# Last f split inside the fifth group's projection, low weight passes last in each first tile, the residual in the output tensor with adding transfers, and a last token tile in three banks

## Chip, cores, metric

One of the eight cores of a Trainium2 chip runs the whole kernel. Its engines are TensorE (PE, matrix products into the accumulation banks of PSUM), VectorE (DVE), ScalarE (ACT) and GpSimd (POOL); SyncE (SP) issues most transfers, GpSimd a few. Every engine works its own list of instructions in order and waits on semaphores for the others. The metric is the time on the device in microseconds for one execution; less is better. The kernel before takes 1384.19 us, the median of three runs (1382.83 to 1386.5).

## The reference

One decoder layer on 1024 tokens of width 1024, float32. What bears on the change is the end: the residual x after the mixer, the convolutional feed-forward block with 2816 channels, and the last norm.

```python
x = x + rms_norm(merged @ w_out[l], norm_mix_post[l])

h = rms_norm(x, norm_ffn_pre[l])
u = causal_dwconv(h @ w_up[l], conv_ffn_w[l])
a, g = jnp.split(u, 2, axis=-1)
f = (jax.nn.gelu(g, approximate=True) * a) @ w_down[l]
x = x + rms_norm(f, norm_ffn_post[l])
```

`rms_norm(x, g)` is `x * rsqrt(mean(x*x) + 1e-6) * g` over the 1024 columns of a token.

## The kernel before

Products are made to nearly float32 accuracy from 16-bit pieces. A float32 tile t, scaled by a power of two s, is split into a high half (float16 of s t, an ACT copy at L86) and a low half (s t less the high half, a DVE operation at L87). A product of two split operands is three matmuls, high x high, high x low and low x high, in the order of `PASSES` = ((0,0), (0,1), (1,0)), the first index for f (or the moving side) and the second for w. The scale comes from a sum of squares over the operand: `scale_of` reduces it on DVE, casts it to bfloat16 (L69), sums it over the partitions by a matmul with one column (`pr`, L74) and shapes the power of two in three small DVE operations (L76 to L79).

The mixer writes the new residual x2 tile by tile, in eight token tiles of 128 x 1024, to a buffer in device memory (`x2d`, L861), about 600 us before the end. The feed-forward block goes through 22 pairs of channel blocks of 128 (an a and a g block each; their matmuls are L1137). What comes out of a pair is a tile `ua` of 128 channels x 1024 tokens. The pairs are gathered in six groups (`GROUPS` = 2, 4, 4, 4, 4, 4), and for each group g there are three steps:

- `f_split(g)` finds the scale over the group's tiles and splits each into `f16` halves (four ACT passes, four DVE passes).
- `dn_split(g)` loads the group's rows of `w_down` (`wd`, L1005) and splits them into `wdh`. Its loads go through four buffers that other weight loads share, so that a load waits until an earlier tile has been split.
- `down(g)` multiplies: for each of eight token tiles and each of two halves of 512 columns, it takes an accumulation bank and runs 3 x GROUPS[g] matmuls (L1036) into it; then the bank is added on DVE to `yacc` (L1042; for the first group ACT copies it, L1040). There are eight banks, shared with the pairs' products and the scales.

`down(g-1)` is called while the pairs of group g are made. At the end come `down(4)`, then `f_split(5)`, then `down(5)`. In the last group each token tile is also finished: ACT squares and sums each half of `yacc` (L1044), DVE multiplies it by the gain (L1046), the two sums are added (L1048), `rstd` makes mean + eps on DVE (L170) and the power of -1/2 on POOL (L171), DVE forms o * r + x2 in two halves (L1052), with x2 loaded back by SP (`x2r`, L1029), and SP stores each half (L1053).

The order of the instructions on each engine is not quite that of the program. A scheduler arranges them when the kernel is built: it takes the program's order as the priority (with some sections raised), and a model of the durations tells it which instruction is ready. In the trace the matmuls of the first tiles of a group are therefore spread over several banks. The order is fixed once the kernel is built; on the chip each engine keeps to it and waits. Large working tiles of the end (`f16`, `wdh`, `ua`, `o`, `x2r`, the gain) share sixteen buffers of 4 KB per partition.

Of the kernel before, what the change touches and what calls it, by code (L numbers as in the profile page):

```python
# [18 lines left out]
F32 = mybir.dt.float32  # L19
I32 = mybir.dt.int32  # L20
AF = mybir.ActivationFunctionType
ALU = mybir.AluOpType
AX = mybir.AxisListType

P = 128
T = 1024
D = 1024
KD = D // P
NH = 512
# [3 lines left out]
GROUPS = (2, 4, 4, 4, 4, 4)  # L33
KH = KD // 2
PASSES = ((0, 0), (0, 1), (1, 0))


class Layer:
# [225 lines left out]
    def mixer(self, mid):  # L264
        tc, nc, a = self.tc, self.nc, self.a
# [446 lines left out]
        with ExitStack() as ph2:  # L712
# [81 lines left out]
            for d in range(1, 8):  # L794
                p = gp[d]
# [37 lines left out]
        self.hA = hA = self.hp.tile([P, 2, KD, T], F16, tag="hT", name="hA")  # L833
        self.hB = hB = self.h7p.tile([P, 2, 3, KH, NH], F16, tag="hB", name="hB2")
        dram = self.top.enter_context(tc.tile_pool(name="dram", bufs=1, space=bass.MemoryType.DRAM))
        self.x2 = [dram.tile([P, D], F32, tag=f"x2_{tt}", name=f"x2d_{tt}") for tt in range(8)]
        gp = self.xp.tile([P, D], F32, tag="x", name="g_post")
        nc.gpsimd.dma_start(gp, a["g_mix_post"].broadcast_to([P, D]))
        gf = self.xp.tile([P, D], F32, tag="x", name="g_ffn")
# [144 lines left out]
    def ffn(self):  # L984
        tc, nc, a = self.tc, self.nc, self.a
        ff0 = self.ff0
        f16, invd, yacc, draw = {}, {}, [None] * 8, self.dsums
        ng = len(GROUPS)

        def f_split(g):  # L990
            smf, ft = smfs[g], fts[g]
            s, inv = self.scale_of(smf, GROUPS[g], keep=True)
            f16[g] = []
            for n, fo in enumerate(ft):
                t = self.slot([P, 2, T], F16, f"f16_{g}_{n}")
                self.split(t, fo, s, f"f{g}_{n}")
                f16[g].append(t)
            invd[g] = inv

        def dn_split(g, wh=False):  # L1000
            s, inv = self.scale_of(draw[g], GROUPS[g], keep=True)
            out = []
            for i in range(GROUPS[g]):
                t = self.ws.tile([P, D], F32, tag="ws", name=f"wd2_{g}_{i}")
                nc.sync.dma_start(t, a["w_down"][ff0[g] + i])  # L1005
                w = self.wh.tile([P, 2, D], F16, tag="wh", name=f"wdh_{g}_{i}") if wh else \
                    self.slot([P, 2, D], F16, f"wdh_{g}_{i}")
                self.split(w, t, s, f"dn{g}_{i}")
                out.append(w)
            draw[g] = out, inv  # L1010

        def down(g):
            w, inv = draw.pop(g)
            sm = self.small(f"sd{g}", keep=True)
            self.mul(sm[:, 0:1], invd[g], inv)
            last = g == ng - 1
            if last:
                gq = self.slot([P, D], F32, "g_ffn_post")
                nc.gpsimd.dma_start(gq, a["g_ffn_post"].broadcast_to([P, D]))
            for tt in range(8):  # L1020
                if g == 0:
                    yacc[tt] = (self.o16p.tile([P, D], F32, tag="o16", name=f"yacc{tt}") if tt < 4 else
                                self.xp.tile([P, D], F32, tag="x", name=f"yacc{tt}"))
                y = yacc[tt]
                if last:
                    o = self.slot([P, D], F32, f"o{tt}")
                    sm_ = self.small(f"fin{tt}")
                    x2 = self.slot([P, D], F32, f"x2r{tt}")
                    nc.sync.dma_start(x2, self.x2[tt])  # L1029
                for nh in range(2):  # L1030
                    ps = self.bank(f"pd{g}_{tt}_{nh}")
                    sl = ds(nh * NH, NH)
                    n = 0
                    for k in range(GROUPS[g]):
                        for hi, wi in PASSES:
                            nc.tensor.matmul(ps, f16[g][k][:, hi, ds(tt * P, P)], w[k][:, wi, sl],  # L1036
                                             start=n == 0, stop=n == 3 * GROUPS[g] - 1)
                            n += 1
                    if g == 0:
                        nc.scalar.activation(y[:, sl], ps, AF.Copy, scale=sm[:, 0:1])  # L1040
                    else:
                        nc.vector.scalar_tensor_tensor(y[:, sl], ps, sm[:, 0:1], y[:, sl], ALU.mult, ALU.add)  # L1042
                    if last:
                        nc.scalar.activation(self.junk(f"jf{tt}_{nh}")[:, sl], y[:, sl], AF.Square,  # L1044
                                             accum_out=sm_[:, 3 + nh:4 + nh])
                        nc.vector.tensor_tensor(o[:, sl], y[:, sl], gq[:, sl], ALU.mult)  # L1046
                if last:
                    nc.vector.tensor_tensor(sm_[:, 0:1], sm_[:, 3:4], sm_[:, 4:5], ALU.add)  # L1048
                    r = self.rstd(sm_)
                    for e in range(2):  # L1050
                        sl = ds(e * NH, NH)
                        nc.vector.scalar_tensor_tensor(o[:, sl], o[:, sl], r, x2[:, sl], ALU.mult, ALU.add)  # L1052
                        nc.sync.dma_start(a["out"][ds(tt * P, P), sl], o[:, sl])  # L1053

        smfs = [self.small(f"sm_f{g}", keep=True) for g in range(ng)]
        fts = [[] for _ in range(ng)]
        prs = self.pairs

        def finish(f):
            g = max(g for g in range(ng) if ff0[g] <= f)  # L1060
            fts[g].append(prs[f].finish(smfs[g][:, f - ff0[g]:f - ff0[g] + 1]))

        for g in range(ng):
            for n in range(GROUPS[g]):
                f = ff0[g] + n
                p = prs[f]
                begun = n == 2 and 1 <= g < ng - 1
                if f >= 1 and not begun:
                    if f >= 2:
                        p.prod(1)  # L1070
                    prs[f - 1].prod(4)
                if f >= 1 and f + 1 < NFF:
                    self.pair_split(f"u{f + 1}")
                if 1 <= f and f + 2 < NFF:
                    self.pair_fetch(f"u{f + 2}")
                if f >= 1 and not begun:
                    finish(f - 1)
                p.prod(6)
                if f >= 2:
                    p.prod(5)  # L1080
                if f >= 2:
                    p.prod(2)
                p.prod(7)
                if n == 1 and g >= 1:
                    f_split(g - 1)
                    if g < ng - 1:
                        dn_split(g - 1)
                p.prod(3)
                if f == 0:
                    self.pair_sums("u2")  # L1090
                if n == 1 and 1 <= g < ng - 1:
                    prs[f + 1].prod(1)
                    p.prod(4)
                    finish(f)
                    down(g - 1)
                if f >= 1 and f + 2 < NFF:
                    self.pair_sums(f"u{f + 2}")
                if n == 2:
                    self.dn_sums(GROUPS[g])
        dn_split(ng - 2)  # L1100
        prs[NFF - 1].prod(4)
        finish(NFF - 1)
        dn_split(ng - 1, True)
        down(ng - 2)
        f_split(ng - 1)
        down(ng - 1)


# [158 lines left out]
```

## Time and profile before

| what | value |
|---|---|
| median of three runs | 1384.19 us (1382.83 to 1386.5) |
| the profiled execution | 1386.05 us |
| span of its instructions | 1384.3 us |
| TensorE occupied | 1340.9 us (97%) |
| VectorE, ScalarE, GpSimd | 1052.5, 836.7, 28.6 us |
| matmuls of the down projection (L1036) | 1056, 232.5 us |
| mean granted TensorE clock | 0.996 |

Times in the profile are microseconds from the start of the span. Occupied time of TensorE counts overlapping matmuls once; a matmul of 512 columns is listed with 379 ns, though another can start about 216 ns after it. A figure in square brackets at the end of a row of the timeline is the time for which the engine sat idle before that row, and what released it. The granted clock is the share of full speed that the power control gave TensorE.

### The profile page before, as it was taken

To read this page: it belongs to the slowest core of one execution; us is meant where nothing else is said; L and a number is where in the kernel's file an instruction comes from. 1 tells how busy PE (TensorE), PEld (TensorE's weight loads), DVE (VectorE), ACT (ScalarE), POOL (GpSimd) and SP (SyncE) were. 2 spreads that over 40 slices of the span, in tenths; PEclk is the share of its full clock that TensorE was granted. 3 is DMA by queue.
4 is the path that set the end of the run, shared out by engine and by line. 5 is a ranking of instruction groups with operands and counts; after the bars stand their busy time and mean duration, and the time that the engine had idled before them with its cause. 6 is when DMAs were issued, how large, how long until landed. Compare 5 with 4: busy or idle time off the path is not lost. (4 is left out here: it accounts for less than half of the span.)

```text
span 1384.3 us, 17016 instructions
## 1 busy us (share of the span) xinstructions
PE 1340.9 (97%) x6639; PEld 607.1 (44%) x6639; DVE 1052.5 (76%) x1646; ACT 836.7 (60%) x1169; POOL 28.6 (2%) x45
## 2 busy tenths in 40 slices
PE   6999999999989999999999999999999999999997
PEld 3444444444434444444454444444444444444443
DVE  5667777776684797878788886985995796699757
ACT  6668777786864465666466576652762662567422
POOL 2000000000000000000010000000000000000001
PEclk9999999999999999999999999999999999999999
DMA  7102111111111112351341223122120322312125
GB/s 260 62 1 61 31 34 39 35 31 31 31 31 46 31 31 61 91 183 39 114 135 49 61 61 122 47 76 91 62 91 3 119 61 62 122 46 107 61 71 188
DMA packets 28593, 99.74 MB, mean 72 GB/s; under 512 B 3296, under 2 KB 3424, under 8 KB 28512
## 3 DMA queue, kind: packets, MB, share of 16 engines
q1 hardware_dynamic: 28080, 97.08, 21.4%
q0 software_dynamic: 432, 1.57, 0.3%
q8 instruction: 52, 0.85, 0.2%
q14 instruction: 29, 0.24, 0.1%
HBM read 90.25 MB, written 8.39 MB: 71 GB/s over the span
## 5 line engine op out<-in xcount | busy, mean ns | idle before, releaser
L1137 PEld LDWEIGHTS <-wh_u 128*128 128x128 f16 x1848 | 178.7, 98 | 217.7 <-issue 4.0
L1036 PE MATMUL pd<-wdh,f 128*128 128x512 f16 x1056 | 232.5, 381 | 9.3 <-DVE wdh L87 5.1
L1036 PEld LDWEIGHTS <-f 128*128 128x128 f16 x1056 | 103.6, 98 | 136.4 <-issue 11.3
L86 ACT ACTIVATE wh_u<-ws_u,sc 128x1024 f16<-128x1024 f32 (+1 forms) x66 | 64.2, 998 | 101.6 <-DVE sc L78 82.0
L1042 DVE SCALAR_TENSOR_TENSOR yacc<-pd,sd,yacc 128x512 f32<-128x512 f32 x80 | 58.7, 748 | 68.1 <-PE pd L1036 60.7
L1137 PEld LDWEIGHTS <-wh_g 128*128 128x128 f16 x588 | 56.8, 98 | 71.5 <-ACT wh_g L86 2.3
L853 PE MATMUL py<-wh_wo,m 128*128 128x512 f16 x384 | 83.9, 379 | 0.0
L87 DVE SCALAR_TENSOR_TENSOR wh_u<-ws_u,sc,wh_u 128x1024 f16<-128x1024 f32 (+1 forms) x66 | 72.0, 1103 | 7.1 <-ACT wh_u L86 7.1
L625 DVE SCALAR_TENSOR_TENSOR w<-zc,w 128x1024 f16<-128x1024 f32 (+3 forms) x48 | 45.7, 955 | 32.0 <-ACT w L624 32.0
L582 PE MATMUL A<-sh,tri 128*128 128x512 f16 (+3 forms) x352 | 67.9, 322 | 0.7 <-DVE zc L620 0.7
L604 ACT ACTIVATE sp<-zc 128x1024 f32<-128x1024 f32 (+3 forms) x48 | 40.2, 838 | 46.4 <-DVE zc L597 29.1
L1214 DVE SCALAR_TENSOR_TENSOR ugu<-cgu,cw_g,ugu 128x1023 f32<-128x1023 f32 (+1 forms) x44 | 56.4, 1282 | 10.9 <-ACT ugu L1212 10.5
L1214 DVE SCALAR_TENSOR_TENSOR ua<-cau,cw_a,ua 128x1023 f32<-128x1023 f32 (+1 forms) x44 | 56.3, 1278 | 1.1 <-ACT ua L1212 1.0
L853 PEld LDWEIGHTS <-m 128*128 128x128 f16 x384 | 37.5, 98 | 44.1
L608 DVE TENSOR_TENSOR sh<-sp,sh 128x1024 f16<-128x1024 f32 (+3 forms) x48 | 45.8, 953 | 12.5 <-ACT sh L607 12.3
L622 ACT ACTIVATE zc<-zc 128x1024 f32<-128x1024 f32 (+3 forms) x48 | 40.1, 834 | 15.2 <-DVE zc L620 14.7
L620 DVE SCALAR_TENSOR_TENSOR zc<-A,zc 128x1024 f32<-128x1024 f32 (+3 forms) x48 | 45.6, 950 | 2.6 <-PE A L582 2.5
L1212 ACT ACTIVATE ua<-cau,cw_a 128x1024 f32<-128x1024 f32 x22 | 25.1, 1139 | 37.1 <-DVE cau L1164 33.9
L56 ACT ACTIVATE jk_u<-ws_u 128x1024 bf16<-128x1024 f32 x44 | 46.3, 1053 | 1.0 <-DMA ws_u<-w_up_nt 0.2
L200 PE MATMUL pk<-hT,wh_k 128*128 128x512 f16 x192 | 46.8, 380 | 0.0
L200 PE MATMUL pq<-hT,wh_q 128*128 128x512 f16 x192 | 44.3, 379 | 1.3 <-DVE sc L79 1.3
L565 PE MATMUL pywc<-p,wh_wc 128*128 128x512 f16 x192 | 43.4, 387 | 2.2 <-ACT p L86 1.6
(613 smaller groups left out, 2626.0 us busy)
## 6 DMA issues: line engine op xcount, KB each, us to landing
ws_u<-w_up_nt SPq DMA_DIRECT2D x44, 512.0 KB, 3.6
ds<-w_down SPq DMA_DIRECT2D x22, 512.0 KB, 6.1
wd<-w_down SPq DMA_DIRECT2D x22, 512.0 KB, 3.7
ws_g<-w_in_nt SPq DMA_DIRECT2D x14, 512.0 KB, 3.6
x<-x SPq DMA_DIRECT2D x8, 512.0 KB, 8.0
ws_wo<-w_out SPq DMA_DIRECT2D x8, 512.0 KB, 7.5
xr<-x SPq DMA_DIRECT2D x8, 512.0 KB, 4.1
x2d<-x SPq DMA_DIRECT2D x8, 512.0 KB, 2.9
```

The costliest lines, as they stand in the source:

```text
L56: self.nc.scalar.activation(self.junk(f"jk_{name}"), src, AF.Square, accum_out=acc)
L86: self.nc.scalar.activation(dst[:, 0, :], src, AF.Copy, scale=s)
L87: self.nc.vector.scalar_tensor_tensor(dst[:, 1, :], src, s, dst[:, 0, :], ALU.mult, ALU.subtract)
L200: nc.tensor.matmul(ps, w[:, wi, ds(k * P, P)], hT[:, hi, k, ds(c * NH, NH)], start=n == 0, stop=n == last)
L582: nc.tensor.matmul(out, w, mv, skip_group_check=True, **kw)
L608: nc.vector.tensor_tensor(sh[:, 1, :, off:], sp[:, :, off:], sh[:, 0, :, off:], ALU.subtract)
L625: nc.vector.scalar_tensor_tensor(w[:, 1, :, off:], zc[:, :, off:], 2.0 ** 14, w[:, 0, :, off:], ALU.mult, ALU.subtract)
L853: nc.tensor.matmul(ps, m16[k][:, hi, ds(tt * P, P)], wo[k][:, wi, sl], start=k == 0 and p == 0, stop=k == 7 and p == 2)
L1036: nc.tensor.matmul(ps, f16[g][k][:, hi, ds(tt * P, P)], w[k][:, wi, sl], start=n == 0, stop=n == 3 * GROUPS[g] - 1)
L1042: nc.vector.scalar_tensor_tensor(y[:, sl], ps, sm[:, 0:1], y[:, sl], ALU.mult, ALU.add)
L1137: nc.tensor.matmul(ps, w[wt][:, wi, ds(wc * NH + k * P, P)], self.block(i, hi, k), start=first and n == 0, stop=n == 3 * KH - 1, skip_grou ...
L1214: nc.vector.scalar_tensor_tensor(u[:, lag:], c[:, :T - lag], sm[:, 2 - lag:3 - lag], u[:, lag:], ALU.mult, ALU.add)
```

## The change

Four things are edited.

1. `f_split(5)` is no longer called between `down(4)` and `down(5)`, but inside `down(4)`, ahead of token tile 5.
2. In token tile 0 of every group, both halves' banks first take the passes with the high half of w for all weight tiles of the group (high f and low f), and then, in a second round, the passes with its low half. The other tiles keep the order of `PASSES`. Both banks of a tile are now taken before its matmuls.
3. The mixer writes x2 of token tiles 0 to 6 into the output tensor itself; tile 7 keeps a buffer of its own. At the end, tiles 0 to 6 are not loaded back: ACT multiplies o by r in one pass of 128 x 1024, and a transfer issued by GpSimd adds o to what stands in the output.
4. In the last group, token tile 7 uses three banks, of 512, 256 and 256 columns, and its three sums of squares are added by one reduction.

```diff
-        self.x2 = [dram.tile([P, D], F32, tag=f"x2_{tt}", name=f"x2d_{tt}") for tt in range(8)]
+        self.x2 = [a["out"][ds(tt * P, P), :] for tt in range(7)] + \
+            [dram.tile([P, D], F32, tag="x2_7", name="x2d_7")]
...
-        def down(g):
+        def down(g, between=None):
...
             for tt in range(8):
+                if between:
+                    between(tt)
...
-                    x2 = self.slot([P, D], F32, f"x2r{tt}")
-                    nc.sync.dma_start(x2, self.x2[tt])
-                for nh in range(2):
-                    ps = self.bank(f"pd{g}_{tt}_{nh}")
-                    sl = ds(nh * NH, NH)
-                    n = 0
-                    for k in range(GROUPS[g]):
-                        for hi, wi in PASSES:
-                            nc.tensor.matmul(ps, f16[g][k][:, hi, ds(tt * P, P)], w[k][:, wi, sl],
-                                             start=n == 0, stop=n == 3 * GROUPS[g] - 1)
-                            n += 1
+                    if tt == 7:
+                        x2 = self.slot([P, D], F32, f"x2r{tt}")
+                        nc.sync.dma_start(x2, self.x2[tt])
+                parts = [(0, NH), (NH, NH // 2), (NH + NH // 2, NH // 2)] if last and tt == 7 else [(0, NH), (NH, NH)]
+                pd = [self.bank(f"pd{g}_{tt}_{nh}")[:, :parts[nh][1]] for nh in range(len(parts))]
+                ks = range(GROUPS[g])
+
+                runs = [[(k, p) for k in ks for p in ((0, 0), (1, 0))], [(k, (0, 1)) for k in ks]] if tt == 0 else \
+                    [[(k, p) for k in ks for p in PASSES]]
+                for run in runs:
+                    for nh, part in enumerate(parts):
+                        for n, (k, (hi, wi)) in enumerate(run):
+                            nc.tensor.matmul(pd[nh], f16[g][k][:, hi, ds(tt * P, P)], w[k][:, wi, ds(*part)],
+                                             start=run is runs[0] and n == 0, stop=run is runs[-1] and n == len(run) - 1)
+                for nh, part in enumerate(parts):
+                    ps, sl = pd[nh], ds(*part)
...
-                    nc.vector.tensor_tensor(sm_[:, 0:1], sm_[:, 3:4], sm_[:, 4:5], ALU.add)
+                    if len(parts) == 2:
+                        nc.vector.tensor_tensor(sm_[:, 0:1], sm_[:, 3:4], sm_[:, 4:5], ALU.add)
+                    else:
+                        nc.vector.tensor_reduce(sm_[:, 0:1], sm_[:, 3:6], AX.X, ALU.add)
                     r = self.rstd(sm_)
+                    if tt < 7:
+                        nc.scalar.activation(o, o, AF.Copy, scale=r)
+                        nc.gpsimd.dma_start(a["out"][ds(tt * P, P), :], o, accum_op=ALU.add)
+                        continue
...
-        down(ng - 2)
-        f_split(ng - 1)
+        down(ng - 2, lambda tt: tt == 5 and f_split(ng - 1))
         down(ng - 1)
```

## The prediction

> **What bounds the kernel now.** I read the page's engine totals first, then who TensorE waits for, then its timeline around those waits, and last the tail behind the final matmul.
>
> ```profile
> PE 1340.9 (97%) x6639; PEld 607.1 (44%) x6639; DVE 1052.5 (76%) x1646; ACT 836.7 (60%) x1169; POOL 28.6 (2%) x45
> ```
>
> TensorE is occupied 1340.9 of 1384.3 us, so time comes only from its 43 us of idle, from its clock, or from the ends of the span. The waits of TensorE (engine line waited for: total us, times, longest) at the down projection's matmul, L1036, are:
>
> ```profile
> PE pd L1036 <- DVE wdh L87: 5.1, 5, 1.6
> PE pd L1036 <- ACT f L86: 2.3, 1, 2.3
> PE pd L1036 <- DVE cau L1164: 1.5, 1, 1.5
> PE pd L1036 <- ACT wdh L86: 0.4, 1, 0.4
> ```
>
> All four belong to starts of a group: the first projects no further until weights or f are split. The 2.3 us is the last group's. The timeline (start, duration, engine, line, operation, tiles, count, idle before and releaser) shows it:
>
> ```profile
> 1290.45 39.87 PE L1036 MATMUL pd<-wdh,f 128*128 128x512 f16 x184 [0.19 <-DVE wdh L87]
> ...
> 1301.36 1.28 DVE L87 SCALAR_TENSOR_TENSOR wdh<-wd,sc,wdh 128x1024 f16<-128x1024 f32 x1 [0.20 <-ACT wdh L86]
> ...
> 1307.70 0.15 DVE L69 CAST rb<-sc 128x1 bf16<-128x1 f32 x1
> ...
> 1328.69 0.58 POOL L1019 DMA_DIRECT2D g_ffn_post<-g_ffn_post  x1 [589.11 <-DVE yacc L1042]
> ...
> 1330.16 0.17 PE L74 MATMUL pr<-rb,ones 128*128 128x1 bf16 x1
> 1331.40 4.27 ACT L86 ACTIVATE f<-ua,sc 128x1024 f16<-128x1024 f32 x4 [25.13 <-DVE sc L78]
> 1332.58 4.87 DVE L87 SCALAR_TENSOR_TENSOR f<-ua,sc,f 128x1024 f16<-128x1024 f32 x4 [0.96 <-ACT f L86]
> 1332.61 43.30 PE L1036 MATMUL pd<-wdh,f 128*128 128x512 f16 x192 [2.27 <-ACT f L86]
> ```
>
> The input of the last f split is complete at 1307.85 (1307.70 + 0.15), yet its one-column matmul stands behind the whole of the fifth group in TensorE's order, so the splits begin at 1331.40 and TensorE idles 2.27 us. The stretches around that gap (us, busy time of each engine, granted clock, share of the DMA engines, GB/s) show a second price:
>
> ```profile
> 1330.33:1332.61 2.28, 0.01 (x2) 0.01 (x1) 1.22 (x6) 1.21 (x2) 0.00 (x0) 1.00 1.02 296
> 1332.61:1336.46 3.85, 3.85 (x10) 1.41 (x11) 3.85 (x4) 3.06 (x3) 0.00 (x0) 0.56 0.77 301
> 1336.46:1375.91 39.45, 39.45 (x183) 17.70 (x181) 31.45 (x58) 10.12 (x28) 4.61 (x7) 1.00 0.45 150
> ```
>
> After 2.28 us of idle the clock is granted at 0.56 for 3.85 us; then it is full again. At 1.00, 183 matmuls in 39.45 us are 0.2156 us each, and the fifth group's 184 in 39.87 agree (0.2167).
>
> **The change, part by part.**
>
> *The last f split moves into the fifth group.* Its instructions stay the same: one reduce, one cast, one one-column matmul, four small DVE operations, four ACT passes (4.27 us) and four DVE passes (4.87 us). They now start ahead of token tile 5, at about 1290.45 + 5 x 24 x 0.216 = 1316.4, after the cast of 1307.85, so the one-column matmul waits for nothing. ACT is empty there (the 25.13 us of idle in its row), and DVE evicts 0.75 us in every 2.59 us. The split is done near 1323, seven us ahead of the last group; cover for it is tiles 5 to 7 (15.5 us of matmuls). Without that cover it would cost again what it costs now. What is removed: the 2.27 us gap, and the slow clock behind it: 43.30 us less 192 x 0.2156 + 0.16 for the pipeline's fill (41.56) = 1.74. Together **4.0 us**. What is late next is nothing: the last group's weights were split by 1302.6 (1301.36 + 1.28), and its buffers come from those free before.
>
> The page TensorE: Matmul & The Clock Gate of the Trainium skill (Part 1, "What's actually happening") puts the fall to half rate after an idle window of about 3.4 us. By that figure a gap of 2.28 us would not slow the clock and only 2.3 us would be won; the trace's 0.56 behind a 2.28 us gap decides against it here.
>
> *Low w passes last, in the first token tile of each group.* The start of the fourth group:
>
> ```profile
> 1136.21 2.17 ACT L86 ACTIVATE wdh<-wd,sc 128x1024 f16<-128x1024 f32 x2
> 1138.14 1.46 PE L1036 MATMUL pd<-wdh,f 128*128 128x512 f16 x6
> 1139.90 1.28 DVE L87 SCALAR_TENSOR_TENSOR wdh<-wd,sc,wdh 128x1024 f16<-128x1024 f32 x1
> 1141.24 5.99 PE L1036 MATMUL pd<-wdh,f 128*128 128x512 f16 x27 [1.64 <-DVE wdh L87]
> ...
> 1144.95 1.15 ACT L86 ACTIVATE wdh<-wd,sc 128x1024 f16<-128x1024 f32 x1 [1.92 <-DMA wd<-w_down]
> 1146.13 1.28 DVE L87 SCALAR_TENSOR_TENSOR wdh<-wd,sc,wdh 128x1024 f16<-128x1024 f32 x1 [0.47 <-ACT wdh L86]
> ```
>
> Six matmuls, I read one in each of six banks, and then 1.64 us until the low half of the first weight tile is there. After the change the first tile's two banks take both passes of the first two weight tiles: 8, plus 4 in other banks, 12 x 0.216 = 2.59 us, to 1140.73; 0.5 us of wait is left to 1141.2. But the low passes of that tile now queue behind high passes of weight tiles three and four, whose load lands only at 1144.95 and whose high half is there at 1146.10. Of the 36 matmuls on two weight tiles in six banks, 32 remain in front: 1138.14 + 0.5 + 6.91 = 1145.55, a new wait of 0.5. Won: 1.64 - 1.0 = 0.6. The other groups start so:
>
> ```profile
> 813.87 0.38 PE L1036 MATMUL pd<-wdh,f 128*128 128x512 f16 x1 [1.47 <-DVE cau L1164]
> 815.06 4.04 PE L1036 MATMUL pd<-wdh,f 128*128 128x512 f16 x18 [0.82 <-DVE wdh L87]
> ...
> 909.41 17.00 PE L1036 MATMUL pd<-wdh,f 128*128 128x512 f16 x78 [0.80 <-DVE wdh L87]
> ...
> 1025.33 17.00 PE L1036 MATMUL pd<-wdh,f 128*128 128x512 f16 x78 [1.65 <-DVE wdh L87]
> ```
>
> The 0.80 can go whole (six extra matmuls are 1.3 us); the 1.65 is the twin of the 1.64 and gives 0.7; the first group gives two matmuls, 0.4, since a bank is what it waits for first; the fifth's 0.19 goes. Sum 0.8 + 0.7 + 0.6 + 0.4 + 0.2 = **2.7 us**. Bounds: 0 (an order of issue that does not use the freedom) to 5.1 (all waits for a low half); a loss is the second rival.
>
> *The tail.* The chain behind the last matmul, which ends at 1375.91:
>
> ```profile
> 1374.04 1.42 DVE L1052 SCALAR_TENSOR_TENSOR o<-o,fin,x2r 128x512 f32<-128x512 f32 x2 [0.73 <-POOL fin L171]
> 1374.82 6.38 SPq L1053 DMA_DIRECT2D out<-o  x4
> 1375.37 0.75 DVE L1042 SCALAR_TENSOR_TENSOR yacc<-pd,sd,yacc 128x512 f32<-128x512 f32 x1
> ...
> 1376.76 0.75 DVE L1042 SCALAR_TENSOR_TENSOR yacc<-pd,sd,yacc 128x512 f32<-128x512 f32 x1
> ...
> 1377.60 0.63 ACT L1044 ACTIVATE jf<-yacc 128x512 bf16<-128x512 f32 x1 [0.67 <-DVE yacc L1042]
> ...
> 1379.43 1.42 DVE L1052 SCALAR_TENSOR_TENSOR o<-o,fin,x2r 128x512 f32<-128x512 f32 x2 [0.73 <-POOL fin L171]
> ```
>
> Tile 7's first half is evicted only at 1375.37, because DVE holds tile 6's final pass, which waited for POOL; its bank was full at 1375.91 - 2.59 = 1373.32. So the second half goes out 0.85 us late. For tiles 0 to 6 that pass moves to ACT as one 128x1024 multiplication, and the x2r loads leave SP. The last bank has 256 columns. Rows for the smaller forms (busy, mean ns):
>
> ```profile
> L335 DVE SCALAR_TENSOR_TENSOR v<-pv,v 128x256 f16<-128x256 f32 x16 | 6.0, 418 | 5.8 <-ACT v L333 5.8
> L1212 ACT ACTIVATE ua<-cau,cw_a 128x1024 f32<-128x1024 f32 x22 | 25.1, 1139 | 37.1 <-DVE cau L1164 33.9
> L56 ACT ACTIVATE jk_u<-ws_u 128x1024 bf16<-128x1024 f32 x44 | 46.3, 1053 | 1.0 <-DMA ws_u<-w_up_nt 0.2
> 250.19 1.26 PE L582 MATMUL A<-sh,tri 128*128 128x256 f16 x8
> ```
>
> The eviction takes 0.42 to 0.75; I take 0.45, near the first. The square then starts 0.55 after the last matmul instead of 1.69 (1377.60 - 1375.91): 1.14 won. The square falls from 0.63 to 0.42 by the slope between 512 and 1024 columns (0.63, 1.05): 0.21. The three-column sum replaces a two-operand one of 0.16; equal. Against that, 24 matmuls of 256 columns: the row's eight give (1.26 - 0.27)/7 = 0.141 us a step where half of 0.216 would be 0.108, so 0 to 0.8, and I take 0.4. Net **0.95 us**.
>
> *Adding transfers.* None is in this trace. Near it stand:
>
> ```profile
> x2d<-x SPq DMA_DIRECT2D x8, 512.0 KB, 2.9
> x2r<-x2d SPq DMA_DIRECT2D x8, 512.0 KB, 3.8
> out<-o SPq DMA_DIRECT2D x16, 256.0 KB, 2.1
> g_ffn_post<-g_ffn_post POOLq DMA_DIRECT2D x1, 512.0 KB, 6.3
> ```
>
> An add moves 512 KB in and out: from 2.9 (a plain write) to 9.2 (POOL queue's 6.3 plus a write). Tile 6 ends on TensorE at 1375.91 - 5.18 = 1370.73; with tile 7's steps it is normed at 1370.73 + 0.85 + 1.83 = 1373.41, scaled by 1374.55. Tile 7's output, issued at 1374.82 + 6.38 - 0.33 = 1380.87, lands at 1383.0 now and 1382.05 then, so the add has 7.5 us. Between 2.9 and 9.2 I take 7.8, nearest to 3.8 + 2.9 on the POOL queue: **0.3 us lost**. On POOL the next tile's power operation stands behind the add's issue (an issue there took 0.58 us) and is ready only some 2 us later, so it is not held. The writing of x to the output instead of another buffer costs nothing: the same 2.9 us transfer, waited for by nobody for 600 us.
>
> **Sum:** 4.0 + 2.7 + 0.95 - 0.3 = 7.35 us. The profiled execution took 1386.05 us (span 1384.3 and 1.7 around it), 1.9 over the median 1384.19 and inside the runs' spread of 1382.83 to 1386.5. On it the sum gives 1378.7; on the mean of these four times, 1384.9, it gives **1377.6**, which I forecast.
>
> **Rivals.** (1) *The split order wins nothing at the group starts*, since the order of issue had already spread over six banks; speaks for it: only six matmuls were in hand in spite of the many that the program offers. Then 4.65 remain: 1380.3. (2) *The run of high passes becomes the wait*: issued as written, TensorE does 8 matmuls (to 1139.87) and waits for weight tile three until 1146.1, 6.2 us in place of 1.64, and a gap of that length brings the slow clock, 1.7 more. Three groups lose 3 x (4.6 + 1.7) = 19 less the 4.65: 1399. It is slower than before from a gap of some 3.2 us per start, or 2.3 with the slow clock. Against it: 78 matmuls in 17.00 us without a gap, although the third weight tile came late, so the order follows arrivals now. (3) *The adds run behind*: they pass one queue, 5.18 us apart. Over 5.2 us of the queue each, they pile up; the first is issued near 1339 (1330.3 + 5.2 for tile 0 + 3.8 for its norm and scaling, as in tile 6), so seven end at 1339 + 7x + 1.3, and from x = 6.3 the kernel is slower; at 9.2, 1405. Against it: 16 engines moved 301 GB/s above, so 1 MB takes 3.5 us. (4) *One add lags*: at 9.2 it ends 1.7 us after tile 7's output; 1379.3 with the other terms, 1380.7 with half of the group starts.
>
> **Chances.** Forecast 0.53 (its own range 1375 to 1379.5), rival 1 0.20, rival 4 0.14, rival 2 0.08, rival 3 0.05. A measurement of this kernel tells about 0.3% from no change, that is 1380.0 to 1388.3. Faster: 0.53 + half of rival 1 + 0.6 of rival 4 = 0.71; slower: most of rivals 2 and 3, 0.11; the same 0.18. Low end 1373.5: all of the 5.1 us won, no loss at 256 columns or adds, on the runs' lower half; high end 1382.5: rival 1 with the lagging add and the runs' upper half.
>
> **What would show it.** The profile after should have no wait of TensorE for ACT's f, clock 1.00 through the last group, a tail of 7 to 7.5 us where it is 8.4 now, group starts whose waits for the low halves shrink from 5.1 us, and adds that land in under 7.5 us. A wait of more than 3 us at a start, for weight tile three, or adds over 9 us would prove me wrong.

## The result and the profile after

The changed kernel takes 1375.89 us, the median of five runs (1373.96 to 1376.65), where the kernel before takes 1384.19 (1382.83 to 1386.5, by now also of five). The ratio is 0.9933, with a 95% interval of 0.992 to 0.9947: 9.3 us less, 7.3 to 11.1. The forecast was 1377.6, with 7.35 us won, in a range of 1373.5 to 1382.5, and 0.71 for faster. In a later comparison on one chip the same kernel gave 0.9934 (0.9922 to 0.9946).

TensorE's waits of the changed kernel (engine, line waited for, total us, times, longest) at the down projection, which is L1043 now:

```profile
PE pd L1043 <- ACT wdh L86: 1.2, 2, 0.7
PE pd L1043 <- DVE cau L1178: 1.0, 1, 1.0
PE pd L1043 <- DVE wdh L87: 0.6, 1, 0.6
```

The wait for ACT's f is gone, and the waits for low halves of w fell from 5.1 us to 0.6. Those for high halves rose from 0.4 to 1.2, since the first group now waits 0.69 us for a high half where it waited 0.82 for a low one. In all 9.3 us of waits at this line became 2.8. The timeline of the changed kernel around the split and the end (start, duration, engine, line, operation, tiles, count, idle before):

```profile
1283.99 26.06 PE L1043 MATMUL pd<-wdh,f 128*128 128x512 f16 x120 [0.47 <-ACT wdh L86]
...
1309.89 0.17 PE L74 MATMUL pr<-rb,ones 128*128 128x1 bf16 x1
1309.92 20.45 PE L1043 MATMUL pd<-wdh,f 128*128 128x512 f16 x94
...
1311.13 4.26 ACT L86 ACTIVATE f<-ua,sc 128x1024 f16<-128x1024 f32 x4 [8.87 <-DVE sc L78]
...
1317.22 1.27 DVE L87 SCALAR_TENSOR_TENSOR f<-ua,sc,f 128x1024 f16<-128x1024 f32 x1
...
1329.77 37.32 PE L1043 MATMUL pd<-wdh,f 128*128 128x512 f16 x184
```

The one-column matmul now runs after 120 matmuls of the fifth group, and the last low half of f is done at 1318.49 (1317.22 + 1.27), some 7 us ahead of the last group. TensorE has no gap from 1283.99 to 1367.09. The stretches of the changed kernel (us, busy time of each engine, granted clock, DMA share, GB/s) say the same of the clock, and give the tail:

```profile
1309.90:1367.09 57.19, 57.19 (x278) 26.93 (x276) 34.86 (x61) 22.89 (x43) 10.71 (x15) 1.00 0.41 74
1367.09:1374.20 7.11, 0.00 (x0) 0.00 (x0) 2.64 (x6) 0.51 (x2) 0.56 (x1) 0.66 0.69 148
```

The clock is 1.00 through the last group, and 7.11 us lie behind the last matmul where there were 8.39. The distances between the first matmuls of the groups, in the timelines of both kernels, show where the rest came from. The third column is the second experiment below.

| stretch, us | before | changed | low passes alone |
|---|---|---|---|
| first to second group's start | 96.00 | 95.43 | 95.46 |
| second to third | 115.07 | 114.11 | 114.11 |
| third to fourth | 115.92 | 114.18 | 114.18 |
| fourth to fifth | 150.24 | 149.17 | 149.19 |
| fifth group's start to the last matmul | 87.53 | 83.10 | 87.17 |
| tail | 8.39 | 7.11 | 8.48 |

The first four rows fell by 4.34 us, the fifth by 4.43, the tail by 1.28. At the first group's start the two executions stand level (811.15 and 811.10), though by different ways: the changed one had a stretch at half clock near 744 us (below), and the one before had come there 1.7 us later. That is 10.05 us on the profiled executions; the medians differ by 8.3.

### The profile page after: what moved, and what is told of

It reads as the page before. It is cut to its first block, busy times and chain, and to the rows that moved or that the text cites. A ratio compares the mean times of both kernels' runs of the same rounds, so it can differ in the third digit from the quotient of the medians.

```text
span 1374.2 us, 17008 instructions
## 1 busy us (share of the span) xinstructions
PE 1339.9 (98%) x6651; PEld 608.3 (44%) x6651; DVE 1044.3 (76%) x1634; ACT 844.3 (61%) x1178; POOL 34.2 (2%) x52
## 3 DMA queue, kind: packets, MB, share of 16 engines
HBM read 86.58 MB, written 8.39 MB: 69 GB/s over the span
## 5 line engine op out<-in xcount | busy, mean ns | idle before, releaser
L1043 PE MATMUL pd<-wdh,f 128*128 128x512 f16 (+1 forms) x1068 | 230.3, 377 | 2.8 <-ACT wdh L86 1.2
L1043 PEld LDWEIGHTS <-f 128*128 128x128 f16 x1068 | 104.4, 98 | 127.1 <-issue 4.1
L1050 DVE SCALAR_TENSOR_TENSOR yacc<-pd,sd,yacc 128x512 f32<-128x512 f32 (+1 forms) x81 | 58.5, 741 | 72.5 <-PE pd L1043 65.0
L605 ACT ACTIVATE sp<-sp,one 128x1024 f32<-128x1024 f32 (+3 forms) x48 | 44.5, 928 | 0.8
```

What stands on the lines that cost most here:

```text
L1043: nc.tensor.matmul(pd[nh], f16[g][k][:, hi, ds(tt * P, P)], w[k][:, wi, ds(*part)], start=run is runs[0] and n == 0, stop=run is runs[-1] ...
```

## The experiments

**The f split alone.** On the kernel before:

```diff
-        down(ng - 2)
-        f_split(ng - 1)
+        down(ng - 2, lambda tt: tt == 5 and f_split(ng - 1))
```

> The kernel before with the last f split alone moved into the fifth group ahead of token tile 5. Theory (gap and clock): the 2.27 us wait before the last group goes, and with it the half clock behind it, so TensorE ends 4.0 us earlier and the time is about 1380.9 where before is 1384.9 (ratio 0.9971); the group starts and the tail stay (7.0 us of waits at L1036 for weights, tail 8.4 us). Rival (the gap alone): the slow matmuls behind the gap have another cause and stay, 2.3 us won (0.9983). Rival (a new wait): the split in the middle delays evictions, TensorE waits for a bank, nothing is won.

Measured: ratio 0.9977 (0.9967 to 0.9987), 3.2 us less (1.8 to 4.6). From the fifth group's start to the last matmul it takes 83.41 us instead of 87.53, 4.1 less; the group starts keep their distances. Its timeline (columns as above) has the last three tiles of the fifth group and the whole last group in one piece:

```profile
1314.84 0.17 PE L74 MATMUL pr<-rb,ones 128*128 128x1 bf16 x1
1314.86 57.14 PE L1038 MATMUL pd<-wdh,f 128*128 128x512 f16 x264
```

264 matmuls of 0.2156 us are 56.9. So nothing new is waited for. The tail fell too, from 8.39 to 7.80 us, which was not expected. Its rows show why: DVE starts tile 6's final pass 2.53 us ahead of the last matmul's end (1372.00), where it was 1.87 before, and evicts the second half of tile 7 only 0.19 us late and not 0.85.

```profile
1369.47 1.41 DVE L1054 SCALAR_TENSOR_TENSOR o<-o,fin,x2r 128x512 f32<-128x512 f32 x2 [0.66 <-POOL fin L171]
...
1372.19 0.74 DVE L1044 SCALAR_TENSOR_TENSOR yacc<-pd,sd,yacc 128x512 f32<-128x512 f32 x1
```

The interval of the times takes in both 4.0 and 2.3, so this run alone doesn't say whether the half clock counts.

**The low passes alone**, the new `runs` for token tile 0 with two banks for each tile:

```diff
+                runs = [[(k, p) for k in ks for p in ((0, 0), (1, 0))], [(k, (0, 1)) for k in ks]] if tt == 0 else \
+                    [[(k, p) for k in ks for p in PASSES]]
```

> The kernel before with the order of passes alone changed (low w passes last in token tile 0 of each group). Theory (12 matmuls in hand instead of 6 at each start): the waits for low halves shrink from 5.1 us to about 0.6 and the time falls by 4.4 to 4.6 us (ratio about 0.9968), as the distances between the group starts of the changed kernel show; the 2.3 us gap before the last group stays. What was predicted was 2.7. Rival (a new wait for weight tile three takes it back): 2.7 or less, with waits of TensorE for ACT wdh of about 0.5 us at three groups.

Measured: 0.9979 (0.997 to 0.9987), 2.9 us less (1.8 to 4.2). The profiled execution won 4.3 us at the starts, just as the changed kernel, and 0.36 us more in the fifth group: 4.65. TensorE's waits at the line are these (releaser: total us, times):

```profile
  ACT f L86: 2.3, 1
  ACT wdh L86: 1.2, 2
  DVE cau L1168: 1.0, 1
  DVE wdh L87: 0.6, 1
```

The gap of 2.3 us stays, the 5.1 us for low halves became 0.6. The start of the fourth group, in the changed kernel's timelines of TensorE and of ACT, shows the mechanism:

```profile
1134.82 2.75 PE L1043 MATMUL pd<-wdh,f 128*128 128x512 f16 x12
1138.12 15.70 PE L1043 MATMUL pd<-wdh,f 128*128 128x512 f16 x72 [0.55 <-DVE wdh L87]
...
1141.64 1.15 ACT L86 ACTIVATE wdh<-wd,sc 128x1024 f16<-128x1024 f32 x1 [1.73 <-DMA wd<-w_down]
```

Twelve matmuls instead of six run ahead of the wait, and 0.55 us of it are left. Both were predicted (12 and 0.5). What was predicted besides, a new wait of 0.5 us for weight tile three, is not there: 72 matmuls go on without a gap, though the tile's high half is there only at 1142.79. Seven banks are open and not six: 12 + 72 matmuls are seven times twelve, and so are the 6 + 78 of the kernel before (the prediction shows the 78 at the second and third group). The seventh takes six more matmuls on the first two weight tiles, so 38 were in hand and not 32; 38 x 0.216 + 0.55 is 8.8 us, and the tile came 8.0 us after the start. At the third group the wait is gone whole, though the prediction took it for the fourth's twin: the first low half is there 2.6 us after the group's start (3.1 in the kernel before), which is just what twelve matmuls last.

That the runs show 2.9 us and the profile 4.65 stays open. The interval, 1.8 to 4.2, holds the 2.7 that was predicted, but neither the 4.4 to 4.6 expected of this run nor what the profile shows. The mean granted clock over the eleven runs is 0.9949 where the kernel before has 0.9955, some 0.8 us by estimate; but the adding transfers alone (below), which take no work from TensorE, have 0.9966, so such means differ by as much for reasons that no run here shows.

**More high passes first**, on the changed kernel:

```diff
-... for k in ks]] if tt == 0 else \
+... for k in ks]] if tt < 3 else \
```

> The changed kernel with low w passes last in token tiles 0, 1 and 2 of each group instead of tile 0 alone. Theory (high passes run out): 24 high passes on two weight tiles and 6 more are in hand, 6.5 us, before the order needs weight tile three, and that comes some 7 to 8 us after the group's first matmul; so TensorE gets a new wait for ACT wdh of about 1 us at each of three starts, and the time is 1 to 3 us over the changed kernel. Rival (more high passes first is better or the same): waits at L1036 no more than 2.8 us in all and the same time.

Measured: 0.9943 (0.993 to 0.9955) of the kernel before, median 1376.26 us; by the times alone not told from the changed kernel. Its TensorE timeline at the second, third and fourth group:

```profile
905.07 6.64 PE L1043 MATMUL pd<-wdh,f 128*128 128x512 f16 x30
912.12 11.81 PE L1043 MATMUL pd<-wdh,f 128*128 128x512 f16 x54 [0.42 <-ACT wdh L86]
...
1019.75 6.64 PE L1043 MATMUL pd<-wdh,f 128*128 128x512 f16 x30
1027.28 11.82 PE L1043 MATMUL pd<-wdh,f 128*128 128x512 f16 x54 [0.88 <-ACT wdh L86]
...
1134.91 6.64 PE L1043 MATMUL pd<-wdh,f 128*128 128x512 f16 x30
1143.26 11.82 PE L1043 MATMUL pd<-wdh,f 128*128 128x512 f16 x54 [1.72 <-ACT wdh L86]
```

Thirty matmuls (four in each of six banks and six in the seventh), then a wait for the third weight tile's high half, as the theory says: 0.42, 0.88 and 1.72 us. The waits for ACT wdh sum to 4.1 us where the changed kernel has 1.2. The distances between the group starts are 0.7 us shorter at the first and 0.6, 1.0 and 1.2 longer at the others: 2.0 us lost in all. This is the second rival of the prediction made real, at a small size: one first tile in that order is enough to bridge the wait for low halves, three use up the work that bridges the load.

**The adding transfers alone**, on the kernel before:

```diff
+        self.x2 = [a["out"][ds(tt * P, P), :] for tt in range(7)] + \
+            [dram.tile([P, D], F32, tag="x2_7", name="x2d_7")]
...
+                    if tt < 7:
+                        nc.scalar.activation(o, o, AF.Copy, scale=r)
+                        nc.gpsimd.dma_start(a["out"][ds(tt * P, P), :], o, accum_op=ALU.add)
+                        continue
```

> The kernel before with the residual in the output tensor and the seven adding transfers alone. Theory: TensorE is not touched; DVE loses tile 6's final pass ahead of tile 7's first eviction, so tile 7's second half is evicted 0.85 us earlier and the tail falls from 8.4 to about 7.5 us; the adds land in about 5.5 us each and are hidden. Ratio 0.9994, not told from 1 by the clock on the wall, but by the tail in the profile. Rival (the adds cost): the last add lands after tile 7's output, tail 8.4 or more.

Measured: 0.9991 (0.9982 to 1.0), which the times hardly tell from nothing, and a tail of 7.21 us against 8.39. The tail is 1.18 us shorter, more than the 0.85 expected. Its last tile is evicted as soon as its bank is full:

```profile
1371.94 0.75 DVE L1044 SCALAR_TENSOR_TENSOR yacc<-pd,sd,yacc 128x512 f32<-128x512 f32 x1 [0.64 <-PE pd L1038]
...
1374.53 0.75 DVE L1044 SCALAR_TENSOR_TENSOR yacc<-pd,sd,yacc 128x512 f32<-128x512 f32 x1 [1.11 <-PE pd L1038]
```

DVE waits for TensorE here and not the other way round; the second eviction starts at the end of the last matmul (1374.49), where it was 0.85 us late before.

**Three banks alone**, on the kernel before:

```diff
+                parts = [(0, NH), (NH, NH // 2), (NH + NH // 2, NH // 2)] if last and tt == 7 else [(0, NH), (NH, NH)]
```

> The kernel before with the last token tile in three banks alone (512, 256, 256 columns). Theory: DVE is the engine that holds the tail up, since tile 6's final pass stands ahead of tile 7's first eviction; with three banks DVE has one operation pair more ahead of the last square, which starts some 0.5 us later and is 0.2 us shorter: tail 8.4 to 8.7 us, nothing won (ratio 1.000). Rival (smaller last bank wins by itself): tail 7.8 us or less.

Measured: 1.0003 (0.9995 to 1.0012), tail 8.57 us against 8.39. A smaller last bank wins nothing while DVE is behind.

**Without the adding transfers**, on the changed kernel (eight buffers, x2r loads and the final pass on DVE for every tile):

```diff
-                    if tt < 7:
-                        nc.scalar.activation(o, o, AF.Copy, scale=r)
-                        nc.gpsimd.dma_start(a["out"][ds(tt * P, P), :], o, accum_op=ALU.add)
-                        continue
```

> The changed kernel with the residual as before (eight buffers, loaded back by SP, final pass on DVE), the other edits kept. Theory: DVE again does tile 6's final pass between tile 7's evictions, so the last square starts about 0.6 us later; tail 7.7 us against 7.1, time 0.6 us more than the changed kernel (1376.5 where that has 1375.9). Rival (the adds cost as much as they save): tail 7.1 or less.

Measured: 0.9928 (0.9915 to 0.9942), median 1374.15 us, tail 7.56. The tail was as expected, but the time was below the changed kernel's first runs. Both were therefore run once more beside each other on one chip:

> The changed kernel itself, beside the next run on one chip. Theory (the slow clock is drawn by the phase of a window, not by the kernel): its times spread over some 2.5 us as before, median 1374 to 1376, tail 7.1 us in the profile.

> The changed kernel with the residual loaded back and summed on DVE as before. Theory: a tail of 7.6 us against 7.1, so the median is 0.5 us over the changed kernel beside it or equal within the spread; the 1.7 us by which it was under the changed kernel's first runs were the slow window behind the wait near 744 us, drawn in those. Rival (the adding transfers cost time elsewhere): its median is again 1.5 us or more under the changed kernel.

Measured: 0.9934 (0.9922 to 0.9946) for the changed kernel, median 1374.66, tail 7.20; 0.994 (0.9926 to 0.9953) without the adds, median 1375.74, tail 7.63. The order turned round, and the tails stayed. So nothing shows that the adds cost time elsewhere. With the other edits in place they win about 0.45 us of tail (7.11 against 7.56, 7.20 against 7.63), which the times can't tell from nothing. Alone they won 1.18: the earlier f split had already taken part of DVE's delay away.

**Two banks again**, on the changed kernel:

```diff
-                parts = [(0, NH), (NH, NH // 2), (NH + NH // 2, NH // 2)] if last and tt == 7 else [(0, NH), (NH, NH)]
+                parts = [(0, NH), (NH, NH)]
```

> The changed kernel with the last token tile in two banks again. Theory: eviction 0.75 instead of 0.48 and square 0.63 instead of 0.42 on the path, less 0.07 us of matmuls: tail 7.5 us against 7.1. Rival (more: the 256-column matmuls cost the 0.4 us that was predicted): end of TensorE 0.4 us earlier, and nothing lost in all.

Measured: 0.9937 (0.9924 to 0.9949), tail 7.16 us against 7.11: lost only 0.05 where 0.4 was expected. Up to the issue of the last store the expectation held. It ends at 1370.06 + 1.00 in the changed kernel, 3.97 us after the last matmul, and at 1371.59 + 1.00 here, 4.45 us after it (1368.14); that is 0.48 us. But the stores then take longer. The transfers' issues (engine, count, size, median us to landing) of the changed kernel, and of this one:

```profile
out<-o POOLq DMA_DIRECT2D x7, 512.0 KB, 5.5
...
out<-o SPq DMA_DIRECT2D x2, 256.0 KB, 2.4
```

```profile
out<-o POOLq DMA_DIRECT2D x7, 512.0 KB, 5.5
...
out<-o SPq DMA_DIRECT2D x2, 256.0 KB, 2.0
```

The store that comes 0.48 us sooner lands in 2.4 us instead of 2.0. Tile 6's add, issued by GpSimd at 1366.06, took 5.7 us, and the first store starts at 1370.06, so the two overlap. But one pair doesn't settle what the small bank is worth. Three more profiles, with low passes last in three tiles (above), with the split at tile 7 (below) and of the changed kernel beside (above), have the same tail: the store's issue ends 3.97 us after the last matmul in each, and the add starts 4.0 us before the store. Their stores landed in 2.2, 2.1 and 2.4 us, and their tails are 6.96, 6.82 and 7.20. With two banks and the adds there are two profiles, 7.16 here and 7.21 with the adding transfers alone. So the small bank wins 0.48 us up to the store each time, and from nothing to 0.4 at the end; what sets the landing no run separated.

**All eight tiles by adds**, on the changed kernel:

```diff
-                    if tt < 7:
+                    if tt < 8:
```

> The changed kernel with token tile 7 also added into the output by a transfer, instead of being loaded back and summed on DVE. Theory (an add costs 5.5 us to landing from its issue, and only cover hides it): behind tile 7's power operation come 1.15 us on ACT, 0.3 us to the issue and 5.5 us of transfer where DVE's pass and a plain store took 0.7 + 0.7 + 2.4: tail about 10 us against 7.1, time 3 us more than the changed kernel. Rival (an add is as fast as a store): tail within 0.5 us.

Measured: 0.9957 (0.9942 to 0.9971), median 1378.85 us, tail 10.31 us: 3.2 us longer than in the changed kernel, as worked out. An add is the slower way to store a tile, and tile 7 has nothing to hide it.

**The gap filled**, on the kernel before:

```diff
         f_split(ng - 1)
+        fill = self.bank("fill")
+        for i in range(10):
+            nc.tensor.matmul(fill, self.hA[:, 0, 0, ds(0, P)], self.hA[:, 0, 1, ds(0, NH)],
+                             start=i == 0, stop=i == 9)
         down(ng - 1)
```

> The kernel before with ten matmuls (2.16 us at full rate) on operands that lie ready and with a result that nobody reads, between the last f split's one-column matmul and the last group's first matmul; nothing is moved. Theory (the clock falls for want of work): the gap stays 2.3 us long but is filled, the clock behind it is granted at 1.00, and 1.7 us are won (ratio 0.9988). Rival (the matmuls behind the gap are slow since f's low halves come late): nothing is won and the first nine or so matmuls still come 0.43 us apart.

Measured: 0.9993 (0.9985 to 1.0002), 1.0 us less (2.1 less to 0.3 more): it holds both nothing and most of what was expected. The clock behind the filled gap is 1.00, but that settles nothing, since two kernels with the open gap kept the full clock as well. Stretches of TensorE (us, busy, clock, DMA share, GB/s), first of the low passes alone, then of the adding transfers alone, then of three banks alone; each the gap, and what follows it:

```profile
1324.35:1326.62 2.27, 0.00 (x1) 1.00 1.02 312
1326.62:1330.40 3.78, 3.78 (x10) 0.57 1.01 387
```

```profile
1330.61:1332.88 2.27, 0.00 (x0) 1.00 0.54 218
1332.88:1336.50 3.62, 3.62 (x17) 1.00 0.37 127
```

```profile
1332.01:1334.29 2.28, 0.00 (x1) 1.00 0.95 287
1334.29:1337.90 3.61, 3.61 (x17) 1.00 0.81 314
```

The same idle time is followed by half clock in two of four profiled executions that have it (before and low passes alone) and by the full clock in the other two. It isn't what the matmuls wait for: 17 of them come in 3.6 us at 1.00, and 10 in 3.8 us at 0.57. And the same is found at another place, behind a wait of 1.79 us that all kernels share near 744 us. Eleven of the fourteen profiles have the slow stretch there; the kernel before, the changed kernel beside and the changed kernel without the adds (its first run) do not. Nor is it the load of the DMA engines, which move next to nothing there. The changed kernel, and the same kernel without the adds:

```profile
743.50:745.00 1.50, 1.04 (x4) 0.92 0.00 0
745.00:748.00 3.00, 3.00 (x8) 0.50 0.00 0
```

```profile
743.50:745.00 1.50, 1.00 (x4) 1.00 0.00 0
745.00:748.00 3.00, 3.00 (x15) 1.00 0.00 0
```

The page TensorE: Matmul & The Clock Gate of the Trainium skill (Part 1, "What's actually happening") has the activity watched in free-running windows of about 3.4 us, with a drop after an idle window. The first agrees with these runs: the slow stretch is 3.4 us long at half rate (3.85 us at 0.56 is 2 x 0.44 x 3.85 = 3.4), and a window whose beginning differs from execution to execution would explain why the same wait is followed by half clock in some only; the windows themselves are in no trace here. The second is too strict, since waits of 1.8 and 2.3 us suffice.

**The split later**, on the changed kernel:

```diff
-        down(ng - 2, lambda tt: tt == 5 and f_split(ng - 1))
+        down(ng - 2, lambda tt: tt == 7 and f_split(ng - 1))
```

> The changed kernel with the last f split ahead of token tile 7 of the fifth group instead of tile 5, so that 5.2 us of matmuls cover it and not 15.5. Theory (cover decides): one-column matmul to first f half 2.3 us, then one f half per 1.06 us on ACT and per 1.28 on DVE: the first halves are there about 2.9 us ahead of the last group, the last ones some 4 us after its start, and the order spreads the matmuls over several banks meanwhile; the wait is below 0.5 us and the clock stays at 1.00: the same time as the changed kernel, or up to 1 us more. Rival (all four tiles must be split before the group can run): a wait of about 3 us and half clock behind it, 4 us more.

Measured: 0.9935 (0.9922 to 0.9948), median 1376.02 us. TensorE never waits for f, with 5.2 us of cover instead of 15.5:

```profile
1320.67 11.60 PE L1043 MATMUL pd<-wdh,f 128*128 128x512 f16 x53
1321.88 4.26 ACT L86 ACTIVATE f<-ua,sc 128x1024 f16<-128x1024 f32 x4 [19.14 <-DVE sc L78]
...
1327.98 1.27 DVE L87 SCALAR_TENSOR_TENSOR f<-ua,sc,f 128x1024 f16<-128x1024 f32 x1
```

24 of these 53 matmuls belong to the fifth group's last tile, so the last group starts near 1325.9, over three microseconds before the last low half of f (1329.25). The split needs only to start early, not to be finished.

This order also shows what adds do when they come close together. The first four were issued at 1343.53, 1344.6, 1347.85 and 1350.85, and landed after 5.5, 9.2, 8.3 and 7.8 us; from 1356 on, 5.2 us apart again, after 5.4 to 5.7. There they still had time, but 9.2 us is what the prediction's fourth rival feared for the last one.

## Why the prediction was right, point by point

- *What bounds the kernel* held: the win came from waits of TensorE, its clock and the tail, and the profile shows no other source.
- *The f split, 4.0 us.* The gap and its 2.27 us went, no wait took its place, and on the profiled pair the stretch from the fifth group to the last matmul fell by 4.43 us. But the term was taken for certain, and 1.74 us of it were the half clock behind the gap in one execution. Runs with the same gap at full clock show that this part comes in some executions only, so that the sum should have had 2.3 us plus a share of 1.7. The f split alone measured 3.2 us, and its profile has 0.6 us of shorter tail in that. In the prediction the trace's one row was set against the 3.4 us that the Trainium skill gives; one execution could not decide that.
- *The low passes, 2.7 us.* Mechanism and first half of the working were right, 12 matmuls ahead of the wait and 0.5 us left; the second half was too dear. The new wait for weight tile three did not come, because seven banks were open and not six. Against the predicted 0.4, 0.8, 0.7, 0.6 and 0.2 us the profile of the low passes alone gave 0.54, 0.96, 1.74, 1.05 and 0.36: half of the error is the third group, which wasn't the fourth's twin. On the profile that is the largest error of the sum, in our favour; the times of that run (2.9 us) don't confirm it.
- *The tail, 0.95 us, less 0.3 for the adds.* Measured 1.28 us. The 1.35 of shorter steps came, but split otherwise than thought: the final pass that DVE lost gave 1.18 us alone and some 0.45 on top of the other edits, the earlier f split 0.59 alone, which the prediction had at nothing, and the small bank from nothing to 0.4. They don't add up, since the first two shorten the same delay of DVE. The 0.4 us for 256-column matmuls did not come: 160 x 0.2156 + 24 x 0.108 + 0.16 are 37.25 us, and the row of the last 184 has 37.32.
- *The adds.* Taken at 7.8 us, they landed in 5.2 to 5.8, so the 0.3 us was not lost: they are hidden, the last one landing over 1 us ahead of tile 7's stores; their issue on GpSimd took 0.88 us and not 0.58. Rivals 3 and 4 needed 6.3 and more than 7.5. The sum of rival 4 has a slip: its lag of 1.7 us is added to the 0.3 that the forecast already holds and should replace it, which gives 1379.0 and not 1379.3.
- *Rival 1* (nothing at the starts) fell with the low passes alone. *Rival 2* did not occur at this size, and does with three tiles.
- The sum was 7.35 us, the medians differ by 8.3, the ratio says 9.3. With the sizes of the profiles it would have been 4.7 at the group starts, 2.3 to 4.0 for the gap and 1.3 of tail, 8.3 to 10.0. That the forecast came so near owes something to luck, since a term taken too high (the half clock for certain) stood against terms taken too low (the starts, the tail). Alone the four edits won 3.2, 2.9, 1.2 and -0.4 us by the times, 6.9 together; the intervals are wide enough for the difference to 9.3.

## What to carry to other kernels

A wait at the start of a stage is cheapest to close by giving the engine more work that doesn't need the late operand, but that work is a stock: count how much lies in hand until the next late operand, since going on past it opens the next wait. A shorter tail needs the edits in the right order: here a smaller last tile won nothing while another engine was still busy with the tile before. Where a term of a sum is a slow clock behind a short gap, look at several executions before it is put down as certain.

## What the runs showed of the hardware

- Waits of 1.8 to 2.3 us of TensorE are followed by 3.4 us at half clock in some executions and not in others, at the same place of the same order of instructions: 1.7 us each. Part of the spread of some 3 us between runs of one kernel is likely this; no run separated it.
- An adding transfer of 512 KB from on-chip memory into device memory landed in 5.2 to 5.8 us (median 5.5) with 0.88 us on GpSimd to issue it, where a plain store of the same size took 2.9. Seven of them some 5.2 us apart did not pile up; issued 1.0 to 3.3 us apart, with the split at tile 7, they landed after 7.8 to 9.2 us.
- Two stores of 256 KB that started 4.0 us after an add landed in 2.1 to 2.4 us (four profiles), and in 2.0 where they started 4.5 us after it (two). In the kernel before, without adds, sixteen such stores took 2.0 to 2.5, so that the adds slow them isn't shown.
